# Handing attention's stages to the scheduler in half steps: a decoder block on one Trainium2 core

## The chip, the cores and the metric

The kernel runs on one core of a Trainium2 chip, in one launch. A core has a matrix engine (TensorE, PE in the profile), a vector engine (VectorE, DVE), an activation engine (ScalarE, ACT), GpSimd (POOL), a queue engine that issues DMAs (SyncE, SP) and 16 DMA engines. Each engine executes its own list of instructions in order, and instructions on different engines wait for one another by semaphores. The metric is the device time of an execution in microseconds (us), as the median of several runs; lower is better.

## The reference

One decoder layer on x of 2048 x 1024 in float32, with eight attention heads of 64 and four pooling groups of 128 channels:

```python
hn = rmsnorm(h, norm1_g)
proj = einsum(hn, w_in)                   # 1024 -> [u_pool 512 | q 512 | k 512 | v 512]
y_pool = pool_mixer(u_pool, pool_w, pool_scale)   # mean over the last 2, 4, 8 or 16 rows, minus the row, times a 128x128 matrix
# attention, strictly causal: A[t,s] = sigmoid(z_ts) * prod_{s<j<t} (1 - sigmoid(z_tj)),  z = q.k / 8
o = stick_breaking_attention(q, k, v)
mixed = concat[rmsnorm(y_pool, pool_out_g), rmsnorm(o, attn_out_g)]
h = h + einsum(mixed, w_out)
h = h + einsum(square(relu(einsum(rmsnorm(h, norm2_g), w_up))), w_down)     # 1024 -> 4096 -> 1024
return rmsnorm(h, final_g)
```

The inverse square root inside each rmsnorm, the running product of the attention weights and the evacuations of matrix products are work for the engines other than TensorE.

## The kernel before

The 2048 rows of x are treated as four tiles of 512 (the index j), held transposed: channels on the 128 partitions, rows along the free dimension. Every dense matrix product is done in three passes over values that are split in a high and a low part (hi by hi, hi by lo, lo by hi), so an output block of 128 x 512 with 1024 input channels takes 8 x 3 = 24 products of 128x512. `products` (line 172) issues them, from lines 177, 178 and 179. `split` makes the two parts: the high one on ScalarE (line 145), the low one on VectorE (line 146).

Four stretches follow one another: the input projection with attention woven in (to about 530 us), the output projection (to about 705 us), the up projection (to about 1305 us) and the down projection with the last norm (to the end). The change concerns the first two.

The program of the first stretches is a list of steps, `prog`. `run` (line 1496) goes through it: it takes the split weights of the step, emits the dense products and their evacuation, lets work that was put off run (`catch_up`), and then calls `advance`, which moves attention on. A step is normally two granules of weights (n = 2), one dense output of 24 products; a step of four is two dense outputs whose products alternate (`emit_two`).

Attention is a generator per tile and pair of heads (`near`, line 693). Its units are half heads of 256 queries: 16 of them per tile. A unit (`near_unit`, line 636) has three stages. In the first, four logit matmuls (lines 616 and 617) go into the tile pz; ScalarE makes two sigmoids, sh and sg; GpSimd masks the diagonal of sg (line 647, affine_select); VectorE forms the running products pc with a scan (line 649) and multiplies sg by them (line 658, or 654 at the first unit of a head of tile 0); GpSimd copies two columns of pc to `left` (line 659). In the second, four transposes (line 663) go into pta, and `split` makes `at` of it. In the third, matmuls with v (line 675) add into po, and at every second unit ScalarE and VectorE sum the halves into ot (lines 633 and 634). The stages of three consecutive units overlap: handing out a unit issues its first stage, the second stage of the unit before and the third of the one before that. The loads of q, k and v of the next head are issued with the first unit of a head.

How fast units are handed out is set by numbers. `advance(units)` adds to an account, state["due"], and takes from the generator as long as the account is above zero; each unit costs 0.27. A dense output adds its ratio, RATIO_FRONT in the input projection (0.15 to 0.4 by thirds of a tile pair) and RATIO_TAIL, 0.6, in the output projection:

```python
def advance(units):
    state["due"] += units
    while state["due"] > 0 and todo:
        try:
            with tc.issue_after(last_mm[0].ins):
                state["due"] -= next(todo[0])
```

What is handed out may be placed behind the dense product that last_mm names, and no earlier. From there a scheduler sets the order on each engine, by priority and its own estimate of when operands are ready. The order on the engines is thus the result of where `advance` is called and what last_mm names.

Other work shares the engines there. `inv_rms` makes an inverse root of a mean square: TensorE sums (pm, line 204), VectorE adds the epsilon (line 212), and then GpSimd runs a chain of fifteen small instructions, each needing the one before (one at line 213, three rounds of lines 220 to 223, a cast at 240 and a difference at 241) to give yr, which TensorE spreads over the partitions (pr, line 230). `pool_group` (line 371) forms the windowed means on VectorE (lines 386 and 389), splits the result pl into pls and multiplies it by the group's matrix (pp, lines 396 to 398).

Of the kernel before, what the change touches and what calls it, by code (L numbers as in the profile page):

```python
# [45 lines left out]
def hymba_block(ctx: ExitStack, tc: tile.TileContext, xT, gains, w_in, pool_w, w_out, w_up, w_down, out):  # L46
    nc = tc.nc
# [105 lines left out]
    raws, grans, last_split, last_mm, last_load = [], [], [None], [None], [None]  # L153
# [8 lines left out]
    def weights(first, n):  # L162

        for i in range(len(grans), min(first + WAHEAD, 2 * len(wlist))):
            load_raw(i // 2)
            hl = wp.tile([P, 2, G, P], F32R, tag="hl", name="hl", align_bytes=256, bufs=WAHEAD)
            last_split[0] = split((hl[:, 0], hl[:, 1]), raws[i // 2][:, i % 2])
            grans.append(hl)
            load_raw(i // 2 + 1)
        return grans[first:first + n]  # L170

    def products(ps, hls, acts, half_behind=None):
        n = len(acts)
        for k, (hi, lo) in enumerate(acts):
            hl, c = hls[k // G], k % G
            with tc.issue_after(marks[half_behind].ins) if half_behind and k == n // 2 else nullcontext():
                nc.tensor.matmul(ps, hl[:, 0, c], hi, start=(k == 0), stop=False)  # L177
            nc.tensor.matmul(ps, hl[:, 0, c], lo, start=False, stop=False)  # L178
            mm = nc.tensor.matmul(ps, hl[:, 1, c], hi, start=False, stop=(k == n - 1))  # L179
        last_mm[0] = mm  # L180

    def add_square(ss, c, first):
        if first:
# [112 lines left out]
    todo, begun, finished, state = [], {}, set(), {"gran": 0, "tick": 0, "due": 0.0}  # L296
# [67 lines left out]
    def dense(j, key, w, evac, behind=None, half_behind=None):  # L364
        where, tag = spare.pop(0) if j == 0 and key == "h" and spare else (psd, "pd")
        ps = where.tile([P, T], F32, tag=tag, name="pd")
        with tc.issue_after(marks[behind].ins) if behind else nullcontext():
            products(ps, w, st[j][key], half_behind)
        done[:] = [done[1], evac(ps)]
# [1107 lines left out]
# [6 lines that stand above are left out]
            except StopIteration:  # L1483
                todo.pop(0)
        if not todo:
            state["due"] = 0.0

    def catch_up(n):
        for _ in range(n):
            with ExitStack() as behind:  # L1490
                for ins in (last_split[0], done[0]):
                    if ins:
                        behind.enter_context(tc.issue_after(ins.ins))
                later.pop(0)()

    def run():
        for n, emit, again in prog:
            if n:
                if again:
                    w = grans[state["gran"] - n:state["gran"]]  # L1500
                else:
                    w = weights(state["gran"], n)
                    state["gran"] += n
                state["tick"] += n
                with ExitStack() as behind:
                    for gate in [g for g in gates if g[0] < state["tick"]]:
                        behind.enter_context(tc.issue_after(gate[1].ins))
                        gates.remove(gate)
                    emit(w)
                catch_up(min(len(later), max(state["pieces"], 2 if len(later) > 8 else 1)))  # L1510
                advance(n / 2 * state["ratio"])
            else:
                emit()
        prog.clear()
# [61 lines left out]
    front(1)  # L1576
    tail(True)
    run()
    ffn()

# [3 lines left out]
    with tc.If(got < count):  # L1584
        wlist.clear(), raws.clear(), grans.clear(), gates.clear(), marks.clear()
        state["gran"], last_split[0], last_mm[0], done[:] = 0, None, None, (None, None)
        open_pools(front_scope)
        open_big(left_scope)
        open_att(att_scope)
        for j in range(NT):  # L1590
            far(j)
        att_scope.close()
        open_last(front_scope, last_scope)
        open_out(out_scope)
        tail(False)
        run()
        ffn()
# [45 lines left out]
```

## Time and profile before

| | |
|---|---|
| median of 3 runs | 1903.87 us (1902.76, 1903.87, 1906.84) |
| profiled execution | 1905.2 us, its span 1903.5 us |
| mean granted clock of TensorE | 0.994 |
| busy, TensorE matmul (PE) | 1869.5 us (98%), 8883 instructions |
| busy, TensorE weight load (PEld) | 1555.5 us (82%) |
| busy, VectorE (DVE) | 1480.9 us (78%) |
| busy, ScalarE (ACT) | 1023.7 us (54%) |
| busy, GpSimd (POOL) | 242.1 us (13%) |
| chain of waits, by engine | PE 45%, DMA 6%, DVE 4%, issue 2%, ACT 1% |

A share of busy time says how full an engine was over the whole span, not which wait ended last. For that one goes to a stretch: the windows show the busy time of each engine and the granted clock in it, the waits name what an engine was idle for and by which instruction it was released, and a timeline shows single instructions in order. In the trace a product of 128x512 starts about 0.23 us behind the one before at the higher clock. Such matmuls overlap, so the duration printed for one is longer than that distance.

### The profile page before, as it was taken

What the parts mean: (1) busy time and instruction counts of PE and PEld (TensorE: products, weight loads), DVE (VectorE), ACT (ScalarE), POOL (GpSimd) and SP (SyncE); (2) the same over time, 40 slices, a digit from 0 to 9 for tenths busy, and PEclk for the clock granted to TensorE, in tenths of its full rate; (3) what the DMA queues carried; (4) which work ended last, traced back from release to release, by engine and by line L of the source; (5) the groups of instructions that cost most, each with busy time, mean ns of one, the idle gap of its engine ahead of it and who ended that gap; (6) DMA issues with size and microseconds to landing.
All of it is one profiled execution on the core that took longest, in us unless ns stands there. A gap on an engine that the chain in (4) does not pass through costs nothing.

```text
span 1903.5 us, 26682 instructions
## 1 busy us (share of the span) xinstructions
PE 1869.5 (98%) x8883; PEld 1555.5 (82%) x8883; DVE 1480.9 (78%) x2151; ACT 1023.7 (54%) x1616; POOL 242.1 (13%) x463
## 2 busy tenths in 40 slices
PE   9999999999999999999999999999999999999997
PEld 7888788888888888778888888887788888888886
DVE  6887799668866976778699988786566677888774
ACT  5565466555544465554557555554332665656543
POOL 0333233223421050000000000000010010020120
PEclk9999999999999999999999999999999999999998
DMA  6686696798788867887899888889999899999752
GB/s 224 204 269 196 191 308 213 239 322 278 272 316 306 296 229 254 284 306 276 286 365 334 313 300 278 301 284 326 378 311 326 289 322 301 334 297 342 290 210 91
DMA packets 222164, 535.91 MB, mean 282 GB/s; under 512 B 26048, under 2 KB 32192, under 8 KB 218176
## 3 DMA queue, kind: packets, MB, share of 16 engines
q1 hardware_dynamic: 217264, 525.46, 79.2%
q0 software_dynamic: 4608, 8.39, 2.4%
q8 instruction: 72, 1.18, 0.3%
q14 instruction: 76, 0.62, 0.1%
q10 hardware_dynamic: 144, 0.26, 0.0%
HBM read 349.46 MB, written 184.55 MB: 281 GB/s over the span
## 4 chain that ended last, share of the span: by engine, by line
PE 45%; DMA 6%; DVE 4%; issue 2%; ACT 1%; POOL 0%; SPq 0%; DVEq 0%; ACTq 0%
PE pb L1274 14%; PE pb L1451 12%; PE pY L1101 10%; PE pZ L1101 5%; PE pX L1101 2%; DMA ar<-sd 1%; DVE hw L146 1%; DMA ar<-sdi 1%; PE pb L1391 1%; DMA t<-in_w_down_dram 1%; DMA su<-hs 0%; DMA sd<-a 0%; DMA td<-t 0%; DMA sdi<-a 0%; DMA b<-in_w_down_dram 0%
## 5 line engine op out<-in xcount | busy, mean ns | idle before, releaser
L1101 PE MATMUL pY<-sa,hw 128*128 128x512 f32 x1536 | 366.3, 389 | 3.0 <-ACT u L1024 2.6
L1101 PEld LDWEIGHTS pY<-sa,hw 128*128 128x128 f32 x1536 | 288.0, 188 | 64.3 <-ACT u L1024 3.9
L1274 PE MATMUL pb<-ad,wd 128*128 128x512 f32 x1344 | 305.1, 389 | 0.3 <-DVE ad L146 0.3
L177 PE MATMUL pd<-h,hl 128*128 128x512 f32 x752 | 299.0, 398 | 3.5 <-DVE acc L813 2.0
L179 PE MATMUL pd<-h,hl 128*128 128x512 f32 x752 | 297.6, 396 | 0.0
L178 PE MATMUL pd<-h,hl 128*128 128x512 f32 x752 | 297.5, 396 | 0.0
L1274 PEld LDWEIGHTS pb<-ad,wd 128*128 128x128 f32 x1344 | 252.2, 188 | 53.1 <-DVE ad L146 0.7
L1451 PE MATMUL pb<-ad,wd 128*128 128x512 f32 x1104 | 253.9, 390 | 2.4 <-ACT ad L145 2.0
L1451 PEld LDWEIGHTS pb<-ad,wd 128*128 128x128 f32 x1104 | 206.5, 188 | 46.1 <-ACT ad L145 2.4
L146 DVE TENSOR_TENSOR ad<-ar,ad 128x1024 fp32r<-128x1024 f32 x160 | 193.9, 1220 | 44.6 <-ACT ad L145 44.2
L145 ACT ACTIVATE ad<-ar 128x1024 fp32r<-128x1024 f32 x160 | 168.2, 1053 | 95.2 <-PE pb L1451 32.0
L1101 PE MATMUL pZ<-sa,hw 128*128 128x512 f32 x768 | 187.0, 390 | 1.1 <-DVE a L1044 1.0
L1101 PEld LDWEIGHTS pZ<-sa,hw 128*128 128x128 f32 x768 | 143.7, 188 | 32.4 <-DVE a L1044 2.6
L177 PEld LDWEIGHTS pd<-h,hl 128*128 128x128 f32 x752 | 142.6, 190 | 31.8 <-issue 2.8
L145 ACT ACTIVATE hl<-raw 128x512 fp32r<-128x512 f32 x168 | 104.2, 631 | 116.2 <-PE pd L179 66.1
L179 PEld LDWEIGHTS pd<-h,hl 128*128 128x128 f32 x752 | 142.5, 189 | 28.2
L178 PEld LDWEIGHTS pd<-h,hl 128*128 128x128 f32 x752 | 142.5, 190 | 26.8
L146 DVE TENSOR_TENSOR hl<-raw,hl 128x512 fp32r<-128x512 f32 x168 | 113.9, 684 | 45.8 <-ACT hl L145 45.5
L1018 ACT ACTIVATE a<-a 128x512 f32<-128x512 f32 x96 | 60.1, 629 | 97.4 <-DVE a L1060 43.0
L146 DVE TENSOR_TENSOR hw<-rt,hw 128x512 fp32r<-128x512 f32 x128 | 86.3, 683 | 26.0 <-ACT hw L145 26.0
L145 ACT ACTIVATE wd<-wq 128x1024 fp32r<-128x1024 f32 x56 | 59.3, 1060 | 76.8 <-PE pb L1274 68.1
L146 DVE TENSOR_TENSOR wd<-wq,wd 128x1024 fp32r<-128x1024 f32 x56 | 68.4, 1221 | 34.2 <-ACT wd L145 34.2
(218 smaller groups left out, 2736.2 us busy)
## 6 DMA issues: line engine op xcount, KB each, us to landing
ar<-sd SPq DMA_DIRECT2D x96, 512.0 KB, 5.7
ar<-sdi SPq DMA_DIRECT2D x64, 512.0 KB, 5.8
rb<-in_w_up_dram SPq DMA_DIRECT2D x30, 1024.0 KB, 6.6
sd<-a SPq DMA_DIRECT2D x104, 256.0 KB, 5.1
raw<-in_w_in_dram SPq DMA_DIRECT2D x50, 512.0 KB, 4.8
sdi<-hr SPq DMA_DIRECT2D x96, 256.0 KB, 5.5
wr<-in_w_down_dram SPq DMA_DIRECT2D x48, 512.0 KB, 5.6
sd<-s SPq DMA_DIRECT2D x88, 256.0 KB, 4.7
```

Source lines behind the costliest of these rows:

```text
L145: nc.scalar.activation(hi, src, AF.Copy)
L146: return nc.vector.tensor_tensor(lo, src, hi.bitcast(F32), ALU.subtract)
L177: nc.tensor.matmul(ps, hl[:, 0, c], hi, start=(k == 0), stop=False)
L178: nc.tensor.matmul(ps, hl[:, 0, c], lo, start=False, stop=False)
L179: mm = nc.tensor.matmul(ps, hl[:, 1, c], hi, start=False, stop=(k == n - 1))
L1018: nc.scalar.activation(t, src, AF.Relu)
L1101: nc.tensor.matmul(t, w[:, wx, c], a[:, ax, c % 2], start=first and c == 0 and x == 0, stop=last and c == G - 1 and x == 2, skip_group_che ...
L1274: nc.tensor.matmul(b, t[:, wx, 2 * (kk % 2) + c, i * P:(i + 1) * P], a[:, ax, c], start=p in ("P1", "P5", "P2") and kk == 0 and c == 0 and ...
L1391: nc.tensor.matmul(b[:, cols], block(t, wx, c, n), a[:, ax, c, cols], start=False, stop=(i == 1 and c == 1 and x == 2), skip_group_check=True)
L1451: nc.tensor.matmul(ps[q, n], block(t, wx, c, n), left_[q][:, ax, c], start=(n_ in ("P1", "P3") and kk == 0 and c == 0 and x == 0), stop=(n ...
```

## The change

`products` now sets last_mm at every third product, and when 12 of the 24 are issued it calls `advance` with half the step's ratio. At the end of a step of two, `run` calls it with the other half. The total per step is the same. In a step of four (`emit_two`), `run` still adds two ratios at the end. The changed file has one line more from line 180 on, so that its lines are numbered one higher than those of before: line 647 is line 648 there.

```diff
--- before.py
+++ after.py
@@ -176,8 +176,9 @@
             with tc.issue_after(marks[half_behind].ins) if half_behind and k == n // 2 else nullcontext():
                 nc.tensor.matmul(ps, hl[:, 0, c], hi, start=(k == 0), stop=False)
             nc.tensor.matmul(ps, hl[:, 0, c], lo, start=False, stop=False)
-            mm = nc.tensor.matmul(ps, hl[:, 1, c], hi, start=False, stop=(k == n - 1))
-        last_mm[0] = mm
+            last_mm[0] = nc.tensor.matmul(ps, hl[:, 1, c], hi, start=False, stop=(k == n - 1))
+            if k == n // 2 - 1:
+                advance(state["ratio"] / 2)
 
     def add_square(ss, c, first):
         if first:
@@ -1508,7 +1509,7 @@
                         gates.remove(gate)
                     emit(w)
                 catch_up(min(len(later), max(state["pieces"], 2 if len(later) > 8 else 1)))
-                advance(n / 2 * state["ratio"])
+                advance((n / 2 if n != 2 else 0.5) * state["ratio"])
             else:
                 emit()
         prog.clear()
```

Where instructions stand now, at the three places of which the prediction speaks. A name's number is the program's running number of a tile.

GpSimd's list at the inverse root near 456 us, before: v_5660 is the root's tile, yr_5675 its result, sg and pc those of two attention units.

```order
L221 TENSOR_TENSOR v_5660<-v_5660 128x4
L647 AFFINE_SELECT sg_5598<-sg_5598 128x2x128
L222 TENSOR_SCALAR v_5660<-v_5660 128x4
L223 TENSOR_TENSOR v_5660<-v_5660 128x4
L659 COPY left3_140<-pc_5591 128x2
L220 TENSOR_TENSOR v_5660<-v_5660 128x4
L221 TENSOR_TENSOR v_5660<-v_5660 128x4
L222 TENSOR_SCALAR v_5660<-v_5660 128x4
L647 AFFINE_SELECT sg_5705<-sg_5705 128x2x128
L223 TENSOR_TENSOR v_5660<-v_5660 128x4
L240 CAST yr_5675<-v_5660 128x4
L241 TENSOR_TENSOR yr_5675<-v_5660,yr_5675 128x4
```

After, at the start of the same chain:

```order
L648 AFFINE_SELECT sg_5598<-sg_5598 128x2x128
L660 COPY left3_140<-pc_5591 128x2
L214 TENSOR_SCALAR v_5660<-v_5660 128x4
L221 TENSOR_TENSOR v_5660<-v_5660 128x4
L222 TENSOR_TENSOR v_5660<-v_5660 128x4
```

and at its end:

```order
L222 TENSOR_TENSOR v_5660<-v_5660 128x4
L223 TENSOR_SCALAR v_5660<-v_5660 128x4
L224 TENSOR_TENSOR v_5660<-v_5660 128x4
L241 CAST yr_5675<-v_5660 128x4
L242 TENSOR_TENSOR yr_5675<-v_5660,yr_5675 128x4
L648 AFFINE_SELECT sg_5705<-sg_5705 128x2x128
L660 COPY left3_140<-pc_5698 128x2
```

The first unit's mask (sg_5598) and copy stand ahead of the chain's first instruction, the second unit's (sg_5705) behind its last; the chain itself is in one piece.

VectorE's list at the same place, before; the root's instruction there is the TENSOR_SCALAR of v_5660, which reads the sums pm and starts GpSimd's chain:

```order
L146 TENSOR_TENSOR qk_5542<-pd_5517,qk_5542 128x512
L727 TENSOR_REDUCE zall_141<-zero_5576 128x1
L146 TENSOR_TENSOR hl_5618<-raw_5515,hl_5618 128x512
L146 TENSOR_TENSOR hl_5711<-raw_5515,hl_5711 128x512
L212 TENSOR_SCALAR v_5660<-pm_5655 128x4
L146 TENSOR_TENSOR at_5492<-pta_5487,at_5492 128x512
L634 TENSOR_TENSOR ot_5484<-ot_5484,po_5401 64x512
L146 TENSOR_TENSOR at_5564<-pta_5559,at_5564 128x512
L649 SCALAR_TENSOR_TENSOR pc_5591<-sh_5596,later_keys_106 128x512
L146 TENSOR_TENSOR qk_5648<-pd_5623,qk_5648 128x512
L658 TENSOR_TENSOR sg_5598<-sg_5598,pc_5591 128x2x255
```

After:

```order
L146 TENSOR_TENSOR qk_5542<-pd_5517,qk_5542 128x512
L146 TENSOR_TENSOR at_5564<-pta_5559,at_5564 128x512
L650 SCALAR_TENSOR_TENSOR pc_5591<-sh_5596,later_keys_106 128x512
L146 TENSOR_TENSOR hl_5618<-raw_5515,hl_5618 128x512
L146 TENSOR_TENSOR hl_5711<-raw_5515,hl_5711 128x512
L659 TENSOR_TENSOR sg_5598<-sg_5598,pc_5591 128x2x255
L213 TENSOR_SCALAR v_5660<-pm_5655 128x4
L635 TENSOR_TENSOR ot_5484<-ot_5484,po_5552 64x512
L146 TENSOR_TENSOR qk_5648<-pd_5623,qk_5648 128x512
L146 TENSOR_TENSOR hl_5714<-raw_5621,hl_5714 128x512
L650 SCALAR_TENSOR_TENSOR pc_5698<-sh_5703,later_keys_106 128x512
L659 TENSOR_TENSOR sg_5705<-sg_5705,pc_5698 128x2x255
```

The first unit's split (at_5564), scan (pc_5591) and multiply (sg_5598) stand ahead of the root's instruction now, the second unit's scan and multiply behind it as before.

VectorE's list ahead of the pool matmuls near 206 us, before; pl_2647 is the pool's input, pls_2649 the low half of its split, which TensorE waits for:

```order
L386 TENSOR_TENSOR s_2643<-s_2641 128x520
L146 TENSOR_TENSOR hl_2819<-raw_2695,hl_2819 128x512
L386 TENSOR_TENSOR s_2645<-s_2643 128x512
L146 TENSOR_TENSOR hl_2822<-raw_2745,hl_2822 128x512
L389 SCALAR_TENSOR_TENSOR pl_2647<-s_2645,u_2635 128x512
L634 TENSOR_TENSOR ot_2795<-ot_2795,po_2662 64x512
L146 TENSOR_TENSOR at_2802<-pta_2798,at_2802 128x384
L649 SCALAR_TENSOR_TENSOR pc_2806<-sh_2811,later_keys_106 128x512
L146 TENSOR_TENSOR pls_2649<-pl_2647,pls_2649 128x512
```

After:

```order
L387 TENSOR_TENSOR s_2643<-s_2641 128x520
L146 TENSOR_TENSOR hl_2819<-raw_2695,hl_2819 128x512
L650 SCALAR_TENSOR_TENSOR pc_2777<-sh_2782,later_keys_106 128x512
L635 TENSOR_TENSOR ot_2766<-ot_2766,po_2662 64x512
L387 TENSOR_TENSOR s_2645<-s_2643 128x512
L659 TENSOR_TENSOR sg_2784<-sg_2784,pc_2777 128x2x255
L727 TENSOR_SCALAR zero_2912<-left0_137 128x16
L146 TENSOR_TENSOR at_2773<-pta_2769,at_2773 128x384
L146 TENSOR_TENSOR hl_2822<-raw_2745,hl_2822 128x512
L390 SCALAR_TENSOR_TENSOR pl_2647<-s_2645,u_2635 128x512
L728 TENSOR_REDUCE zall_141<-zero_2912 128x1
L146 TENSOR_TENSOR pls_2649<-pl_2647,pls_2649 128x512
```

A scan, a halves' sum, a multiply, a small compare and a split of attention now stand between the weight split hl_2819 and pl_2647; between pl_2647 and pls_2649 only a small reduction is left.

## Rows read from the trace of the kernel before

**Rows 1.** The page, busy time, share of the span and instructions of each engine:

```profile
PE 1869.5 (98%) x8883; PEld 1555.5 (82%) x8883; DVE 1480.9 (78%) x2151; ACT 1023.7 (54%) x1616; POOL 242.1 (13%) x463
```

**Rows 2.** Windows: length, then busy us by engine, granted clock, DMA share, GB/s:

```profile
200.00:250.00 50.00, 46.70 (x238) 39.18 (x237) 35.45 (x56) 26.77 (x50) 10.47 (x25) 0.93 0.76 238
...
300.00:350.00 50.00, 48.96 (x282) 41.29 (x281) 47.48 (x73) 32.14 (x59) 19.67 (x35) 1.00 0.69 212
350.00:400.00 50.00, 48.70 (x265) 41.23 (x264) 34.32 (x51) 26.35 (x48) 12.61 (x31) 1.00 0.82 259
...
450.00:500.00 50.00, 48.03 (x253) 40.72 (x252) 43.70 (x63) 31.73 (x58) 23.10 (x34) 0.93 0.83 277
...
550.00:600.00 50.00, 48.21 (x229) 40.15 (x228) 36.77 (x60) 25.43 (x44) 7.79 (x30) 1.00 0.99 382
```

**Rows 3.** Timeline of TensorE, 213 to 216 us: start, duration, instruction:

```profile
213.13 0.63 PE L177 MATMUL pd<-h,hl 128*128 128x512 f32 x1
213.56 0.63 PE L178 MATMUL pd<-h,hl 128*128 128x512 f32 x1
...
215.60 0.39 PE L179 MATMUL pd<-h,hl 128*128 128x512 f32 x1
215.83 0.39 PE L177 MATMUL pd<-h,hl 128*128 128x512 f32 x1
```

**Rows 4.** Waits of TensorE, 0 to 750 us: total us, times, longest:

```profile
PE pp L396 <- ACT pls L145: 2.9, 3, 2.1
PE pd L177 <- DVE acc L813: 2.0, 2, 1.8
PE pr L230 <- POOL yr L240: 1.7, 1, 1.7
...
PE pp L397 <- DVE pls L146: 1.4, 2, 1.2
PE ptv L440 <- ACT vf L437: 1.3, 1, 1.3
...
PE pd L177 <- DVE qk L146: 0.8, 1, 0.8
```

**Rows 5.** Timeline of TensorE, 456 us:

```profile
456.20 0.33 PE L230 MATMUL pr<-identr,yr 128*128 128x128 f32 x1 [1.68 <-POOL yr L240]
```

**Rows 6.** Timeline of GpSimd, 449 to 454 us:

```profile
449.02 0.19 POOL L213 TENSOR_SCALAR v<-v 128x4 int32<-128x4 int32 x1 [5.77 <-DVE v L212]
...
450.42 1.43 POOL L220 TENSOR_TENSOR v<-v 128x4 f32<-128x4 f32 x1
...
452.07 0.41 POOL L647 TENSOR_SCALAR_AFFINE_SELECT sg<-sg 128x256 f32<-128x256 f32 x1
...
453.20 1.12 POOL L659 COPY left<-pc 128x2 f32<-128x2 f32 x1
```

**Rows 7.** Timeline of GpSimd, 229 to 234 us:

```profile
229.71 0.19 POOL L213 TENSOR_SCALAR v<-v 128x4 int32<-128x4 int32 x1 [2.31 <-DVE v L212]
...
233.80 0.19 POOL L240 CAST yr<-v 128x4 fp32r<-128x4 f32 x1
```

**Rows 8.** Timeline of VectorE, 450 to 452 us:

```profile
450.64 1.21 DVE L649 TENSOR_TENSOR_SCAN pc<-sh,later_keys 128x512 f32<-128x512 f32 x1
```

**Rows 9.** Timeline of VectorE, 203 to 208 us:

```profile
203.93 0.69 DVE L146 TENSOR_TENSOR hl<-raw,hl 128x512 fp32r<-128x512 f32 x1 [0.42 <-ACT hl L145]
204.54 0.69 DVE L389 SCALAR_TENSOR_TENSOR pl<-s,u 128x512 f32<-128x512 f32 x1
205.14 0.67 DVE L634 TENSOR_TENSOR ot<-ot,po 64x512 f32<-64x512 f32 x1
205.74 0.54 DVE L146 TENSOR_TENSOR at<-pta,at 128x384 fp32r<-128x384 f32 x1
206.20 1.21 DVE L649 TENSOR_TENSOR_SCAN pc<-sh,later_keys 128x512 f32<-128x512 f32 x1
207.34 0.88 DVE L146 TENSOR_TENSOR pls<-pl,pls 128x512 fp32r<-128x512 f32 x1
```

## The prediction

> **What bounds the kernel now.** I read the page first: TensorE is busy for 1869.5 of 1903.5 us [rows 1]. So the change, which hands the same instructions to the engines in another order, can pay only in the 34 us in which TensorE is idle and in the stretches in which its clock is low. Next I read the windows of the stretch in which attention is woven into the dense groups [rows 2]: two windows of 50 us have a granted clock of 0.93, their neighbours 1.00. Each lost 0.07 x 50 = 3.5 us. What that is stands in the timeline [rows 3]: products that start 0.43 us apart (213.13 to 213.56) and then 0.23 us apart (215.60 to 215.83), the lower of the two levels of 1.2 and 2.4 GHz and then the higher. Both low stretches begin just behind a wait of TensorE, so I read the waits third [rows 4]. Of the idle time of the first 750 us six waits matter: the pool matmuls at 206 us (2.1 and 1.2 us, for the two halves of a split), the spread of an inverse root at 456 us (1.7 us, for GpSimd), and three others of 1.8, 1.3 and 0.8 us. The clock fell behind the first pair and behind the 456 us one; it did not fall in the windows that hold the 1.3 us wait (359 us) and the 1.8 us wait (583 us) [rows 2]. The ceiling of any gain is therefore some 9 us of waits and 7 us of low clock.
>
> **What the change is.** Of the engines' instructions none is added or removed; the two orders hold the same rows. In TensorE's the first difference stands near 121 us and the last near 615 us, so everything from the late tail of the output projection on, the up and the down projection, costs what it did. In between, a dense output's 24 products are now cut at 12, and of every two attention units one goes out 12 products, 12 x 0.23 = 2.7 us, earlier. Attention's own DMA loads move with it, on the queue that SyncE issues, by the same 2.7 us; none of the waits [rows 4] is for a load, so I price these at nothing. What can change the time is where the moved units' vector and GpSimd instructions now stand in those engines' queues.
>
> **Place 1, the root at 456 us.** Before, GpSimd's chain for one inverse root runs from 449.02 us until TensorE is released at 456.20: 7.2 us [rows 5, 6]. The same chain with nothing inside takes 4.3 us (229.71 to the end of the cast at 233.99) [rows 7]. The 2.9 us more are three attention instructions inside it (two masks of 0.41 us, as the one at 452.07, and a copy of 1.12) and chain instructions that took longer than their usual 0.20 (the one at 450.42 took 1.43). That one ended at 451.85, with the scan that VectorE ran from 450.64 to 451.85 [rows 8]; the copy too shares its time with a scan. After the change the order has no attention instruction inside this chain: mask and copy of the first unit stand ahead of it, the second unit's mask behind it. The chain starts later, because the vector instruction that begins it now stands behind the first unit's multiply, 0.7 us. I count 4.3 us at best, and at worst 6.3, with the second unit's scan, its multiply and a weight split still holding it for 2 us as the longer ones did; I take 5.2, nearest to the known mean of both. From 449.02 + 0.7 = 449.7 the release then comes at 454.9 (454.0 to 456.0). TensorE reached this point at 456.20 - 1.68 = 454.5, and by its order has 0.3 us more to do before it (a group of logits more, some products fewer), so 454.8: the wait is 0.1 us, at most 1.2. I take 0.3. Since single waits of 1.3 and 1.8 us did not lower the clock, the low stretch behind it goes too. Gain 1.4 + 3.5 = 4.9 us; with the bounds, from 0.5 (wait 1.2, clock falls all the same) to 5.2.
>
> One rule of the Trainium skill speaks for a long hold: by "SBUF — State Buffer", section "SBUF: two separate sides", a vector instruction with two SBUF inputs and a GpSimd instruction that reads SBUF take one port pair in turn, and the later one waits for the whole of the earlier. The trace agrees here, with 1.43 against 0.20 us and the common end at 451.85. By that rule the chain is not safe when attention's instructions leave it, since scan and multiply on VectorE still cross it; the sum would then be nearer to the 6.3 us end.
>
> **Place 2, the pool matmuls at 206 us.** VectorE is nearly back to back here (one gap, 0.42 us) and its split releases TensorE [rows 4, 9]. TensorE's work up to this point is the same in both orders. But the order of VectorE now has five attention instructions ahead of the vector instruction that makes the pool's input (L389): a scan, a halves' sum, a multiply, a small compare and a split. By the distance of starts these take 1.14, 0.60, 0.6 (as the sum), 0.1 and 0.46 = 2.9 us [rows 9], less the gap, 2.5 us. Three of their kind stood between L389 and the second half of the split (205.14 to 207.34, 2.2 us), so that second half is hardly later: the first half comes later and the second follows it at once. Both waits together were 3.3 us. The last one's release moves by 2.5 - 2.2 = 0.3 us at least and by 2.5 at most; I take +1.0, since ScalarE, which splits the first half, is freer there. The low clock stays as it is, 3.5 us.
>
> **Place 3, the rest.** The evacuation of queries and keys at 254.8 us, waited for 0.8 us [rows 4], now stands with other attention work around it; by the order VectorE's run of attention work ahead of it begins earlier, so I let this wait mostly go: -0.6 (0 to -0.8). The waits of 1.3 us (v's transpose) and of 1.8 us (the accumulation at 583 us) have the same instructions directly around them: 0. Where units are no longer handed out two together, their logits, scans and masks spread out, and the time from logits to transposes shrinks by up to 2.7 us at its shortest places. The cover there is VectorE's slack: it is thin only where it is busy 47.5 of 50 us, from 300 to 350 us [rows 2]. If the cover fails, one place costs a wait of some 2.5 us as at place 2; I take 0 and keep it for the range.
>
> **Sum.** -4.9 + 1.0 - 0.6 = -4.5 us on the profiled execution's 1905.2 (span 1903.5 and 1.7 around it), so 1900.7. The median of the runs shown is 1903.9, 1.3 below the profiled one; on that scale the forecast is 1899.4.
>
> **Rivals.**
> *The root keeps its wait.* The three attention instructions leave, but the start 0.7 us later and the scan that crosses the chain give it back. For it: half of the 2.9 us excess was longer chain instructions, not inserted ones. Against it: two of the four vector instructions that crossed it (scan and multiply of the first unit) now stand ahead of its start. Then nothing is gained there: +1.0 - 0.6 on 1903.9, so 1904.3, or 1902.8 if only the wait shrinks by 1.5 and the clock still falls.
>
> *VectorE's queue becomes the bound: slower.* Attention's four vector instructions of a unit (scan, multiply, split, sum, some 2.9 us together, as above) come to stand ahead of an evacuation or a pool split that TensorE needs, in the stretch from 283 to 340 us, as they already do at 206 us. Each such place would cost 2.5 us of wait and a low stretch of 3.5, so 6.0. For it: 47.5 of 50 us busy. Against it: of before's waits only 0.8 us in all is for an evacuation of queries and keys [rows 4], so the others have slack left, of a size that no wait shows. One such place beside the forecast gives 1905.4, no difference; from two on it decides, 1899.4 + 12.0 = 1911.4.
>
> *The change does not do what it says.* The orders differ at all three places, with moved rows on TensorE from 121 to 615 us: chance 0.
>
> *More than forecast.* The wait at 206 us goes as well, since the unit's logits no longer stand directly ahead of it; -7.8 more (its 3.3, the 3.5 and the 1.0 counted), 1891.6. Against it: five more vector instructions in the way.
>
> **How the numbers follow.** Forecast 0.55, with 1896 to 1902.5 as its own range (place 1 complete and place 2 unchanged at the low end, the wait of place 1 still 1.2 us and one small new wait at the high end). The root keeps its wait 0.27. VectorE 0.15. More 0.03. What a measurement of this kernel can tell from no change is 0.2%, 3.8 us: below 1900.1 counts as faster, above 1907.7 as slower. Of the forecast's 0.55 I put 0.40 below 1900.1, since its centre is under that bound and its upper part needs a leftover wait; of the root's rival 0.01. Faster 0.40 + 0.01 + 0.03 = 0.44, same 0.15 + 0.26 = 0.41, slower 0.15. The range reaches from 1895 to 1908, into the bound of VectorE's case, and leaves out its two-place end and the 0.03.
>
> **What would show it.** In the profile after: the granted clock of the window from 450 to 500 us at 1.00 and no wait of the pr spread for GpSimd there over 0.5 us (place 1); the chain between 4.3 and 6.3 us with no mask or copy inside; the waits at 206 us together 3.6 to 5.8 us, still followed by a low clock (place 2); no wait for qk near 255 us; the same idle time from 700 us on. I am wrong if a third window falls to 0.93, if the pr wait stays above 1.2 us, or if a wait of over 2 us shows between 283 and 340 us.

## The result, and the profile after

| | before | after |
|---|---|---|
| median of 20 runs, us | 1903.41 (1898.31 to 1910.54) | 1906.80 (1904.00 to 1913.08) |
| ratio after to before | | 1.0024 (95% interval 1.0016 to 1.0032) |
| profiled execution, us | 1905.20 | 1905.07 |

The change makes the kernel slower by 0.24%, 4.6 us (3.0 to 6.1). The ratio is estimated from all the runs and is not that of the two medians, which are 3.4 us apart; the means are 4.3 us apart. A second series of the same order gave 1.0018 (1.0005 to 1.0031). The forecast was 1899.4, faster. The two profiled executions are of equal length: that of before lies above the median of its runs, that of after below its own. So for either order a second profile was taken, and what follows rests on all four.

The page's line of busy times answers to [rows 1]:

```profile
PE 1868.1 (98%) x8883; PEld 1554.1 (82%) x8883; DVE 1482.3 (78%) x2151; ACT 1022.2 (54%) x1616; POOL 233.3 (12%) x463
```

The same instructions, and busy times within 1.5 us but for GpSimd, whose instructions were held up less (in the second pair of profiles it is 240.4 us before and 229.3 after). The windows of after, with the columns of [rows 2]:

```profile
200.00:250.00 50.00, 46.01 (x238) 38.46 (x238) 35.73 (x57) 25.99 (x48) 11.61 (x24) 0.93 0.78 245
...
300.00:350.00 50.00, 47.94 (x274) 40.65 (x272) 47.47 (x71) 30.88 (x57) 22.46 (x28) 1.00 0.64 207
350.00:400.00 50.00, 48.24 (x266) 40.87 (x266) 32.97 (x49) 24.83 (x46) 13.65 (x36) 1.00 0.80 256
...
450.00:500.00 50.00, 49.37 (x276) 41.68 (x276) 45.31 (x66) 33.63 (x63) 16.12 (x37) 1.00 0.93 308
...
550.00:600.00 50.00, 46.94 (x217) 39.05 (x216) 33.31 (x54) 21.70 (x38) 7.85 (x30) 0.97 0.95 350
```

The window at 450 us is at full clock now, as forecast. But a new window has a lower one: 550 to 600 us, 0.97, with TensorE busy 46.94 us where it was 48.21. The waits of TensorE in the first 750 us of after, as [rows 4] (line numbers one higher):

```profile
PE pp L397 <- ACT pls L145: 4.0, 1, 4.0
PE pd L177 <- ACT sq L188: 3.1, 1, 3.1
...
PE ptv L441 <- ACT vf L438: 1.5, 1, 1.5
PE pta L664 <- DVE sg L659: 1.4, 1, 1.4
PE pd L177 <- DVE qk L146: 1.1, 1, 1.1
...
PE pp L398 <- DVE pls L146: 0.7, 1, 0.7
```

The wait for GpSimd is gone from the top of the list. The second row, at 583 us, stands in place of before's 1.8 us there and names another releaser; the fourth row shown, at 335 us, is new.

To see where time goes between two orders one lays the same dense product of both side by side. From the starts of the products of the first line of `products` I take the time of eight stretches (limits in us of before's first profile: 64.8, 193.9, 296.6, 396.7, 432.4, 494.1, 550.1, 627.4, 690.7):

```
                 65-194 194-297 297-397 397-432 432-494 494-550 550-627 627-691   sum
before            129.2   102.7   100.1    35.7    61.7    56.0    77.3    63.3  626.0
before, again     129.2   101.4   100.3    35.7    60.6    56.0    77.1    63.2  623.4
after             129.3   105.7   100.3    36.4    57.0    55.7    80.2    63.3  627.9
after, again      128.9   105.6   100.6    36.4    55.4    55.7    80.2    64.1  626.9
```

A limit can cut through moved attention work, so a single column holds some work of its neighbours; sums from the left are safer. Up to 494 us after stands 0.5 us ahead of before (mean of two each: 427.8 against 428.3), up to 550 us 0.8 us ahead. From 550 to 691 us it loses 3.5. Together +2.7 us. The rest of the measured 4.6 the traces can't place: outside these columns two executions of one order differ by up to 2.7 us (start to the first limit 64.8 against 65.2 in before, 64.4 against 67.1 in after; from the last limit to the end of TensorE's last product 1202.2 against 1204.0 in before).

### The profile page after: what moved, and what is told of

It is laid out like the page before. It is cut to its first block, busy times and chain, and to the rows that moved or that the text cites. A ratio compares the mean times of both kernels' runs of the same rounds, so it can differ in the third digit from the quotient of the medians.

```text
span 1903.3 us, 26656 instructions
## 1 busy us (share of the span) xinstructions
PE 1868.1 (98%) x8883; PEld 1554.1 (82%) x8883; DVE 1482.3 (78%) x2151; ACT 1022.2 (54%) x1616; POOL 233.3 (12%) x463
## 4 chain that ended last, share of the span: by engine, by line
PE 48%; DMA 6%; DVE 3%; issue 1%; ACT 1%; POOL 0%; SPq 0%; DVEq 0%; ACTq 0%
PE pb L1275 14%; PE pY L1102 12%; PE pb L1452 12%; PE pZ L1102 6%; PE pX L1102 3%; DMA ar<-sd 1%; DMA ar<-sdi 1%; DMA hn<-hs 1%; PE pb L1392 1%; DMA su<-hs 0%; DMA td<-t 0%; DVE hw L146 0%; DMA sd<-a 0%; DMA b<-in_w_down_dram 0%; DMA t<-in_w_down_dram 0%
```

## The experiments

All but two of those on the placing use one switch in the changed kernel: the seven zones are the thirds of the two tile pairs of the input projection (0 to 5) and the output projection (6), and half steps are used only in the zones of HALF (FRAC is 0.5).

```diff
-            last_mm[0] = nc.tensor.matmul(ps, hl[:, 1, c], hi, ...)
-            if k == n // 2 - 1:
-                advance(state["ratio"] / 2)
+            mm = nc.tensor.matmul(ps, hl[:, 1, c], hi, ...)
+            if state.get("zone", 0) in HALF:
+                last_mm[0] = mm
+                if k == n // 2 - 1:
+                    advance(state["ratio"] * FRAC)
+        last_mm[0] = mm
```

The step's end adds the other half in those zones and the whole ratio elsewhere. Lines of these kernels stand 2 to 6 higher. Two theories were set against each other: the queue theory (attention stands ahead of what TensorE needs on VectorE, at several places) and the root theory (what is gained at 456 us is given back later).

**One part alone.** HALF = (0, 1, 2):

> Half steps only in the first tile pair of the input projection (thirds 0 to 2, to about 238 us); from there on whole steps as before. Queue theory (VectorE's queue with attention ahead of what TensorE needs costs the time, at several places): the wait at 206 us grows by about 0.7 us as in the full change, no other new wait, +0.5 to +2 us. Root theory (what is gained at the 456 us root is given back later, the rest is nothing): 0 within 1 us. If most of the +4.6 us of the full change sits here, both fall.

Measured 0.9983 (0.9972 to 0.9995), faster by 3.2 us: neither theory had that. HALF = (3, 4):

> Half steps only in the thirds 3 and 4 of the input projection (about 238 to 412 us). Queue theory: the new waits of the full change at 320 us (0.7) and 335 us (1.4) and a longer one at 256 us are here: +2 to +4 us, the wait at 456 us with its low clock stays as before. Root theory: within 1 us of before.

Measured 1.0002 (0.9990 to 1.0014), -1.9 to +2.7 us, which does not tell the two theories apart. The trace has a longer wait at 255 us and one of 1.5 us at 339, as the queue theory would have it, but the wait at 456 us, which that theory kept, is gone. HALF = (5,):

> Half steps only in the last third of the input projection (about 412 to 494 us), which holds the root at 456 us. Queue theory: this is where the change gains: -3 to -5 us, with the GpSimd wait under 0.5 us and the window 450 to 500 us at full clock. Root theory: the same gain at 456 us in the trace, but the wait at 583 us in the output projection grows by what was gained, so 0 to -1.5 us in the time.

Measured 0.9988 (0.9975 to 1.0000), between the two: the root's wait only fell to 1.3 us, and the wait at 580 us grew to 2.3 with a low clock behind it. HALF = (6,):

> Half steps only in the output projection (from about 494 us). Queue theory: few attention units are left there, within 1 us of before. Rival (the loss is in the output projection itself: one instruction more or less ahead of the evacuation at 583 us lengthens that wait and lowers the clock): +3 to +5 us, wait at 583 us of about 3 us as in the full change.

Measured 1.0007 (0.9993 to 1.0020), which decides nothing, and the trace says why: the instructions of TensorE, VectorE, ScalarE and GpSimd stand in it in the order of before from the first to the last, by names and shapes. Half steps in the output projection alone move nothing, and this kernel is a third execution of before's order. Its wait at 583 us is 1.7 us, as there; that one of 1.9 us came at 673, with 3.4 us of low clock, shows how far executions of one order differ. The other three parts add up to -3.2 + 0.4 - 2.3 = -5.1 us, and the whole is +4.6. So they are not independent, and the table says why:

```
                 65-194 194-297 297-397 397-432 432-494 494-550 550-627 627-691
zones 0,1,2       128.9   102.9    99.2    35.7    56.2    56.1    76.8    62.8
zones 3,4         129.2   105.1   103.1    36.6    54.3    56.7    76.8    63.9
zone 5            129.1   101.5   100.0    35.6    60.0    55.8    79.5    62.8
zone 6            129.2   102.5   100.1    35.7    62.1    56.0    77.2    66.5
```

The root at 456 us is freed by zones 0 to 2 alone and by zones 3 and 4 alone; it can be freed only once. Zones 3 and 4 show a cost of the kind that the queue theory names: some 6 us from 194 to 397 us beyond before (208.2 against 202.2), of which 2.3 are waits and 2.6 low clock; the rest can be moved work. It is seen in the waits of TensorE from 190 to 700 us of that kernel:

```profile
PE pp L402 <- ACT pls L147: 3.6, 2, 2.1
PE pd L179 <- DVE acc L819: 1.8, 2, 1.3
PE po L681 <- ACT at L147: 1.6, 1, 1.6
```

The second pool wait of the first row, 1.5 us at 339 us, was 0.4 in before, and a low stretch follows it: its window 300 to 350 has a clock of 0.97. But the root's gain pays for all that. The same root in the kernel with zones 0 to 2, GpSimd's timeline:

```profile
448.46 0.20 POOL L219 TENSOR_SCALAR v<-v 128x4 int32<-128x4 int32 x1 [7.01 <-DVE v L218]
...
451.92 0.40 POOL L653 TENSOR_SCALAR_AFFINE_SELECT sg<-sg 128x256 f32<-128x256 f32 x1
...
455.17 0.66 POOL L246 CAST yr<-v 128x4 fp32r<-128x4 f32 x1
```

Here four attention instructions are inside the chain, one more than in before, and TensorE does not wait. The chain starts 0.8 us behind the sums (447.6), where before it started 2.4 us behind them, and TensorE comes to the spread 9.1 us behind them instead of 7.9. Here the chain's start and TensorE's other work counted, not what stands in the chain.

**Both orders once more.** HALF empty, and all seven zones:

> No half steps at all: the same instructions in the same order as before, for a second profile. Ratio 1.000 within 0.1%. Queue theory needs the low clock behind the 456 us wait to be there in this profile too; if it is missing, part of what the root gains in the pair of profiles is luck of one execution.

Measured 0.9995 (0.9979 to 1.0012). The wait at 456 us was 2.2 us and the low clock was there, but shorter: 3.4 us instead of 6.8 behind either wait, a clock of 0.97 in both windows. Two more kernels have before's order up to 494 us, zone 6 alone and before with the other placing (below); in both the low clock behind either wait was 6.8 us again. So in four profiles of this order it was 6.8 us three times and 3.4 once: the low clock at the root belongs to the order, and its length varies from execution to execution.

> Half steps everywhere: the same instructions in the same order as the full change, for a second profile. Ratio 1.0015 to 1.0032. Both theories: waits at 206 us of about 4.0, at 320 to 340 us of about 2, at 583 us of about 3 us again; the low stretch behind 583 us is 3.4 or 6.8 us.

Measured 1.0018 (1.0005 to 1.0031): these waits came again (4.0 at 206, 0.7 at 323 and 1.4 at 337, 3.06 at 584), and so did the 3.4 us of low clock behind the last.

**All but one part.** HALF = (0, 1, 2, 5, 6) and HALF = (0, 1, 2, 3, 4, 5):

> Half steps everywhere but in the thirds 3 and 4 of the input projection (238 to 412 us). Queue theory (those thirds cost 3 to 5 us through VectorE's queue, and the root's gain stays): -3 to -5 us. Rival (the loss is made in the output projection, at 583 us): still +1 to +4 us.

Measured 1.0030 (1.0015 to 1.0044), +5.7 us: the queue theory's -3 to -5 fails, and the rival's place too, since TensorE does not wait at 583 us here. The waits from 190 to 700 us show another schedule, with the root unfreed and a new wait in the output projection:

```profile
PE pp L402 <- ACT pls L147: 4.2, 2, 4.0
PE pm L210 <- DVE ss L194: 2.5, 1, 2.5
PE pd L179 <- DVE acc L819: 1.8, 1, 1.8
PE pr L236 <- POOL yr L246: 1.5, 1, 1.5
```

Behind the 2.5 us wait, at 557 us, the clock was low for 6.8 us. Leaving the costly zones 3 and 4 out thus did not take their cost off; it changed what followed.

> Half steps everywhere but in the output projection. Queue theory: the cost of thirds 3 and 4 stays, the loss at 583 us goes: 0 to +3 us. Rival (the loss is made at 583 us, where the evacuation stands behind two instructions more): -1 to -4 us.

Measured 1.0001 (0.9990 to 1.0013). With the output projection in whole steps the wait at 583 us is 1.5 us, the clock stays high there, and the column 550 to 627 is 77.1 us as in before. Its other columns are those of after (105.5, 100.7, 36.4, 56.9). So the loss of the full change shows in the output projection, and the input projection comes out about even: the queue theory's range (0 to +3), at its lower end. It is not the output projection's half steps by themselves, since alone they move nothing (zone 6).

**The evacuation at 583 us.** VectorE's timeline of before there:

```profile
573.57 2.08 DVE L262 SCALAR_TENSOR_TENSOR nt<-ol,gains,ra 128x512 f32<-128x512 f32 x3
575.56 0.69 DVE L146 TENSOR_TENSOR hl<-raw,hl 128x512 fp32r<-128x512 f32 x1
576.16 5.39 DVE L828 SCALAR_TENSOR_TENSOR acc<-acc,gains,r 128x512 f32<-128x512 f32 x8
581.47 0.68 DVE L146 TENSOR_TENSOR h<-nt,h 128x512 fp32r<-128x512 f32 x1
582.07 0.68 DVE L813 TENSOR_TENSOR acc<-pd,acc 128x512 f32<-128x512 f32 x1
```

and of after:

```profile
572.92 2.07 DVE L263 SCALAR_TENSOR_TENSOR nt<-ol,gains,ra 128x512 f32<-128x512 f32 x3
574.91 5.38 DVE L829 SCALAR_TENSOR_TENSOR acc<-acc,gains,r 128x512 f32<-128x512 f32 x8
580.21 0.69 DVE L146 TENSOR_TENSOR hl<-raw,hl 128x512 fp32r<-128x512 f32 x1
580.81 1.29 DVE L146 TENSOR_TENSOR h<-nt,h 128x512 fp32r<-128x512 f32 x2
582.01 0.69 DVE L814 TENSOR_TENSOR acc<-pd,acc 128x512 f32<-128x512 f32 x1
```

TensorE's rows of the wait, before and after:

```profile
582.90 0.47 PE L177 MATMUL pd<-h,hl 128*128 128x512 f32 x1 [1.79 <-DVE acc L813]
582.85 0.76 PE L177 MATMUL pd<-h,hl 128*128 128x512 f32 x1 [3.06 <-ACT sq L188]
```

The last row of either VectorE list is the evacuation that frees the bank for the next dense output. In both a run of eight scalings (5.4 us) stands ahead of it. Behind the run, before had one instruction, after has three; so the evacuation ends at 582.7 in both, though the run ended 1.2 us earlier and TensorE, further on in its work, was idle from 579.8 instead of 581.1. After's row names a square on ScalarE; that square ends at 582.76, but it does not touch the bank: the evacuation, done at 582.70, is the one that counts. TensorE starts 0.15 us behind the end of this evacuation in all four profiles.

Counted from the first limit, TensorE came here 1.0 and 0.5 us earlier in after (first and second pair of profiles) and was let go 0.3 and 1.0 us later. So the longer wait gives back a lead, as the root theory has it, and adds a later evacuation; the low clock behind it comes on top. Zone 5 alone, with the output projection in whole steps, has the same rows in the same order behind the run as after; its wait of 2.3 us, its low stretch and its column of 79.5 go with that.

To test this, the work that is put off in the output projection is placed behind the evacuation of the same step instead of the one before:

```diff
-                for ins in (last_split[0], done[0]):
+                for ins in (last_split[0], done[1] if state["pieces"] == 3 else done[0]):
```

In the full change, in before, and with zones 0 to 2 (there together with the switch):

> The full change, and in the output projection the put-off vector work is placed behind the evacuation of the same step instead of the one before. The evacuation that TensorE waits for at 583 us then stands directly behind the run of eight scalings and one weight split, without the splits of the norm between, and without the three norm products ahead of the run. Theory (the loss of the full change is mostly this evacuation): the 3.1 us wait falls under 1 us and the low clock behind it goes, so 3 to 5 us faster than the full change: ratio to before 0.9990 to 1.0010. Rival (the wait only moves, since VectorE's work of the output projection stays the same): still 1.0018 or more, with a new wait of 2 to 3 us between 583 and 690 us.

Measured 1.0002 (0.9989 to 1.0014), as expected. VectorE's timeline:

```profile
573.16 5.39 DVE L829 SCALAR_TENSOR_TENSOR acc<-acc,gains,r 128x512 f32<-128x512 f32 x8
578.47 0.68 DVE L146 TENSOR_TENSOR hl<-raw,hl 128x512 fp32r<-128x512 f32 x1
579.07 0.68 DVE L814 TENSOR_TENSOR acc<-pd,acc 128x512 f32<-128x512 f32 x1
```

The norm's products and splits are out of the way, the evacuation comes 2.9 us earlier, and TensorE does not wait there at all. A smaller wait, 0.7 us at 611 us with 3.4 us of low clock, takes some of it back: column 550 to 627 is 78.4, against 80.2.

> The kernel before with the same placing of the put-off work. Control: its wait at 583 us is 1.6 to 1.8 us and has no low clock behind it, so there is less to win: -1 to -2 us (ratio 0.9990 to 0.9995). If it wins 3 us or more, the placing helps for another reason and says nothing on the change. Rival: 0 or slower.

Measured 0.9986 (0.9975 to 0.9997), -2.7 us (-4.8 to -0.6), more than expected. That is under the 3 us that would have spoken against the test, but the interval does not exclude them. Column 550 to 627 is 75.2 instead of 77.2, 2 us. So the placing helps either order, and it does not single out what the change costs: with it in both, column 550 to 627 still differs by 3.2 us (78.4 against 75.2), of which the wait at 611 us and its low clock are 2.4, and the means of the 12 runs are 1.8 us apart (by my estimate from their spread, -0.7 to +4.2).

> Half steps only in the first tile pair of the input projection, the best part so far (ratio 0.9983), with the same placing of the put-off work. If the two act at different places they add: wait at 576 us from 1.3 to under 0.5 us, ratio 0.9973 to 0.9983. Rival: the wait moves on, 0.9983 to 0.9995.

Measured 0.9974 (0.9963 to 0.9984), 1898.07 us: faster than before by 4.9 us and than the full change by some 9. They add (0.9983 x 0.9986 = 0.9969), within the intervals. This is the fastest version found.

## Why the prediction was wrong

- **What bounds the kernel: right.** TensorE's time in the eight columns apart from waits and low clock hardly changed. In the first pair 626.0 - 12.0 of waits - 6.8 lost to the clock is 607.2, and 627.9 - 14.6 - 5.1 is 608.2; in the second pair it is 607.6 and 607.5.
- **Place 1, the root: right.** I forecast an uninterrupted chain, a wait of 0.3 us and no low clock. After:

```profile
453.94 0.19 POOL L214 TENSOR_SCALAR v<-v 128x4 int32<-128x4 int32 x1 [1.32 <-DVE v L213]
...
457.55 0.70 POOL L241 CAST yr<-v 128x4 fp32r<-128x4 f32 x1
458.34 1.00 POOL L242 TENSOR_TENSOR yr<-v,yr 128x4 fp32r<-128x4 f32 x1
459.29 0.40 POOL L648 TENSOR_SCALAR_AFFINE_SELECT sg<-sg 128x256 f32<-128x256 f32 x1
```

The chain takes 4.3 us to the end of the cast, the low end of my 4.3 to 6.3, with the second mask behind it. It starts 1.1 us later behind its sums (3.5 us against 2.4), where I had 0.7. A wait of 0.48 us is left, for the difference, which took 1.00 us instead of 0.20 and ended with the second unit's scan on VectorE, at 459.34 and 459.35:

```profile
457.52 0.69 DVE L146 TENSOR_TENSOR hl<-raw,hl 128x512 fp32r<-128x512 f32 x1 [2.22 <-ACT hl L145]
458.13 1.22 DVE L650 TENSOR_TENSOR_SCAN pc<-sh,later_keys 128x512 f32<-128x512 f32 x1
```

The cast, 0.70, ended with the weight split in the same way. The rule cited in the prediction (the Trainium skill, "SBUF — State Buffer", section "SBUF: two separate sides") is thus borne out again: a hold can stay when attention's own instructions leave the chain, but here it fell on the last two and cost 0.5 us. In the second profile, and in the two other kernels that have after's order up to 494 us (half steps everywhere but in the output projection; the full change with the other placing), cast and difference take 0.20 us and TensorE does not wait there. The low clock is gone in all four. My reason for that (waits of 1.3 and 1.8 us had none behind them) was weaker than I took it to be: with zone 5 alone a wait of 1.3 us at this place had 3.4 us of low clock behind it. By its column the gain is 4.7 us in the first pair of profiles (61.7 - 57.0) and 5.1 in the second; by waits and low clock it is 4.9 and 4.2; I had said 4.9.
- **Place 2, the pool matmuls: right.** Forecast +1.0; the waits of 3.3 us became one of 4.0, +0.7. The first half of the split is late and the second follows without a wait, as worked out.
- **Place 3, the evacuation of queries and keys: wrong in sign.** Forecast -0.6; it went from 0.8 to 1.1.
- **Place 3, "VectorE's slack" as a cover, taken at 0: too low.** In the stretch that was named as thin, the waits from 320 to 340 us went from 1.0 to 2.1, one of them for a multiply of attention; 0.3 to 0.6 appeared at a root near 388 us. Together with the two points above this makes +2.4 where the sum had +0.4. It did not reach the slower rival's case of two places at 6.0 each: no low clock followed.
- **The step that failed: "the waits of 1.3 us (v's transpose) and of 1.8 us (the accumulation at 583 us) have the same instructions directly around them: 0".** True of the first (1.3 to 1.5). At the second the order of VectorE had changed in two instructions, and TensorE arrived earlier. The wait grew from 1.7 to 3.1 us (means of two profiles), and in both profiles of after a low stretch followed, 3.4 us at half speed, 1.7 us lost: +3.1 us. I had listed this place's wait, and its instructions could have been read in the order; I read TensorE's neighbours and not those of the evacuation that it waits for. With whole steps in the output projection this one term is gone (column 550 to 627 at 77.1 instead of 80.2) and the time is 1.0001: that is shown. The other placing takes the wait away too, but it makes before faster as well, so it does not prove the term's share of the time. That the remaining 2 us between the traces' +2.7 and the measured +4.6 have a cause of their own is not shown; it stays open.

So the sum, by means of two profiles each: the root -4.6 (waits -2.0, low clock -2.6), other waits of the input projection +2.4, low clock at 206 us +0.9 (6.8 us in both profiles of after, 6.8 and 3.4 in those of before), 583 us +3.1: +1.8 of the +2.7 that the columns show, the rest in smaller waits and in TensorE's own time. The +0.9 at 206 us is chance, not a price of the change: in four profiles of either order up to 494 us the low stretch there was 6.8 us three times and 3.4 once. Over the same four and four the root gives -5.2 (waits -2.2, low clock -3.0). The forecast had the gain and missed the price. My slower rival had the right engine, VectorE, and the wrong place; none of the three signs that I had named as showing me wrong came.

## What to carry to other kernels

A change to when work is handed out is judged at every wait of the bounding engine in the stretch that it reshuffles, by reading what now stands ahead of the *releaser* in its own queue; the place where it helps is only one of them. Gains of parts don't add when they are one gain: test the whole, and the whole less one part. Where put-off vector work can run in a block ahead of an evacuation, placing it behind the evacuation of the same step was worth 2.7 us here (0.6 to 4.8) with no change in the work. And a variant is evidence only if it moves something: lay its instruction lists beside those of the kernel that it should differ from, as zone 6 alone shows.

## What was not expected of the hardware

The clock stretch behind one and the same wait is not the same in each execution: behind the 3.3 us at 206 us it was low for 6.8 us in three of the four profiles of before's order up to there and for 3.4 us in one. Waits of 1.3, 1.5 and 1.8 us had none behind them in before and after, 3.06 us had 3.4 in both profiles of after; but in the kernel with zone 5 alone a wait of 1.3 us at 456 us had 3.4 too, and with the full change and the other placing two waits of 0.4 and 0.3 us at 611 us had 3.4. The length of a wait alone thus does not say whether the clock falls.
